# A decoder layer on one core: w1 and w3 of the second SwiGLU by Strassen's seven block products for features 4 to 21

## The chip, the cores and the metric

The kernel runs on one core of one Trainium2 chip. The metric is the device time of one execution in microseconds (us), as the median of several runs; lower is better.

## What is computed

One decoder layer on 512 tokens of 1024 features, float32 in and out. Two gated feed-forward blocks (SwiGLU) stand around a mixer of a diagonal state-space branch (S5) and a gated linear attention (GLA):

```python
def swiglu(x, w1, w3, w2):
    return (jax.nn.silu(x @ w1) * (x @ w3)) @ w2

h = h + 0.5 * swiglu(rms_norm(h, ffn1_norm[l]), ffn1_w1[l], ffn1_w3[l], ffn1_w2[l])
...
h = h + 0.5 * swiglu(rms_norm(h, ffn2_norm[l]), ffn2_w1[l], ffn2_w3[l], ffn2_w2[l])
out = rms_norm(h, final_norm)
```

w1 and w3 are 1024 x 2816, that is 22 tiles of 128 features; w2 is 2816 x 1024. In what follows a *feature* is one of these 22 tiles.

## The kernel before, in words

All activations lie feature-major: 128 features on the partitions, the 512 tokens along the row, so h is eight tiles of 128x512. Each float32 operand is split into two parts, `hi` (the value rounded to TensorE's format, written by ScalarE) and `lo` (the rest, subtracted by VectorE), and a product is three passes on TensorE: hi by hi, hi by lo and lo by hi (`mm3`, L208). `gemm` (L213) adds these over the tiles of the contraction into one PSUM bank.

The weights come as a stream of *units* (class `Unit`): one piece of 128x1024 or less, with its load on the SP queue, its split, its products (`mm`) and what follows on the other engines (`post`). The main loop (L1298) goes through the units in the order of the list and for each one issues the load of the unit five ahead, the products, the split of the unit three ahead, and the post. This loop is what sets the order on every engine: each engine works off its own queue in that order and waits by semaphores. There are five load buffers (`raw`), four `hi`, four `lo`, four PSUM banks `mm`, four `sp`, and 63 slots of 128x512 (`g`) for everything else.

`ffn` (L249) writes the units of a SwiGLU. For each feature there is a unit of w1 and one of w3, 24 products of 128x512 each (8 tiles by three passes); `g_post` (L253) makes the gate: two multiplications by the norm's factor out of PSUM, Silu on ScalarE, their product, its hi and lo. The second SwiGLU goes through the features in groups of 6, 6, 6 and 4 (`GROUPS2`). After each group come eight units of w2, one per tile of h, which add that group's share to h. The last group goes half of the tokens after half, with products of 128x256 (`tail_units`, L1166), since the final norm of the first half then runs beside the products of the second. Helpers record most operations, so VectorE's two-operand operations have L65, its scalar-tensor-tensor ones L77, ScalarE's L86, and TensorE's three passes L209 to L211.

Of the kernel before, what the change touches and what calls it, by code (L numbers as in the profile page):

```python
# [15 lines left out]
P = 128  # L16
# [4 lines left out]
GROUPS2 = [6, 6, 6, 4]  # L21
# [11 lines left out]
class Ring:  # L33
    def __init__(self, items):
        self.items = items
        self.n = 0

# [23 lines left out]
def _body(nc, a, sb, pp):  # L61
# [63 lines left out]
    def newton(y, v, t):  # L125
        """y = 1 / sqrt(v)."""
# [50 lines left out]
    def finish_h(m, g, norm):  # L177
        """hi and lo of h g for the next product, and the sum of squares; the DVE's share one tile later."""
# [40 lines left out]
    units = []  # L219

    def load(n):
# [3 lines left out]
        u.raw = raws.get()  # L225
        if u.load is not None:
            u.load(u)
        else:
            nc.sync.dma_start(out=u.raw[:, 0:u.width], in_=u.src)

    def split(n):
# [3 lines left out]
        if u.split is not None:  # L235
            u.split(u)
            return
# [3 lines left out]
        sub(u.lo[:, 0:w], u.raw[:, 0:w], u.hi[:, 0:w].bitcast(F32))  # L241

# [6 lines left out]
    def ffn(w1, w3, w2, groups, norm_key, lead, finish_tile, tail=False):  # L249
# [15 lines left out]
        for q, nk in enumerate(groups):  # L265
            last = q == len(groups) - 1
            for f in range(c0, c0 + nk):
# [17 lines left out]
                ua.early = ub.urgent and tail and last  # L285
                units.extend([ua, ub])
            if tail and last:
                tail_units(w2, c0, nk, gs)
                continue
            for m0 in range(0, KT, 2):  # L290
# [45 lines left out]
    for _ in range(WARM):  # the tensor engine's clock is at half until it has worked for a while  # L336
        PE.matmul(bank[:, 0:P], lhsT=idle, rhs=idle, start=True, stop=True)

    def lead1(ua, ub, pa, pb):
# [3 lines left out]
        ua.load = ub.load = no  # L343
# [3 lines left out]
        def mm():  # L347
            for u in (ua, ub):
                u.hi, u.lo = his.get(), los.get()
# [1025 lines left out]
```

## Time and profile before

| | |
|---|---|
| median of three runs | 1089.84 us (1089.45 to 1090.64) |
| span of the profiled execution, first to last instruction | 1085.4 us |
| the profiled execution's own time | not listed beside its span; the median is 4.4 us above the span |
| TensorE busy | 1070.3 us, 4968 products |
| VectorE busy | 626.8 us |
| ScalarE busy | 384.0 us |
| GpSimd busy | 68.8 us |
| mean granted TensorE clock | 0.994 of full speed |

How to read it: the span is what the profiler saw of one execution. Products are pipelined and their ends are modelled, so a single one is recorded longer (some 390 ns for 128x512) than the distance between two starts; what a product costs in a stream is the distance of the starts. The second SwiGLU takes about the last 375 us of the span.

### The profile page before, as it was taken

What the parts mean: (1) busy time and instruction counts of PE and PEld (TensorE: products, weight loads), DVE (VectorE), ACT (ScalarE), POOL (GpSimd) and SP (SyncE); (2) the same over time, 40 slices, a digit from 0 to 9 for tenths busy, and PEclk for the clock granted to TensorE, in tenths of its full rate; (3) what the DMA queues carried; (4) which work ended last, traced back from release to release, by engine and by line L of the source; (5) the groups of instructions that cost most, each with busy time, mean ns of one, the idle gap of its engine ahead of it and who ended that gap; (6) DMA issues with size and microseconds to landing.
All of it is one profiled execution on the core that took longest, in us unless ns stands there. A gap on an engine that the chain in (4) does not pass through costs nothing.

```text
span 1085.4 us, 12968 instructions
## 1 busy us (share of the span) xinstructions
PE 1070.3 (99%) x4968; PEld 892.2 (82%) x4968; DVE 626.8 (58%) x1164; ACT 384.0 (35%) x605; POOL 68.8 (6%) x121
## 2 busy tenths in 40 slices
PE   9999999999999999999999999999999999999996
PEld 7888888888888898888788888888888888888885
DVE  6688654896643637685585654655344444444446
ACT  6323254222222532654644333433222222322224
POOL 4003500100400000001000000000000000000001
PEclk9999999999999999999999999999999999999998
DMA  7323223421521332122131323323242233314112
GB/s 275 102 62 128 96 79 88 134 75 49 169 74 49 131 98 84 52 79 78 59 98 59 98 96 97 98 80 90 81 136 88 63 122 98 97 45 151 59 39 78
DMA packets 33228, 101.31 MB, mean 93 GB/s; under 512 B 3968, under 2 KB 5440, under 8 KB 33168
## 3 DMA queue, kind: packets, MB, share of 16 engines
q1 hardware_dynamic: 32256, 99.17, 28.9%
q0 software_dynamic: 480, 0.79, 0.3%
q8 instruction: 39, 0.64, 0.2%
q10 hardware_dynamic: 432, 0.54, 0.1%
q14 instruction: 21, 0.17, 0.1%
HBM read 98.19 MB, written 2.10 MB: 92 GB/s over the span
## 4 chain that ended last, share of the span: by engine, by line
PE 95%; ACT 2%; DVE 2%; DMA 1%; issue 0%; SPq 0%; DVEq 0%; ACTq 0%
PE mm L209 28%; PE mm L211 28%; PE mm L210 28%; ACT g L86 1%; DVE g L65 1%; PE sp L949 1%; PE sp L951 1%; PE sp L950 1%; PE mm L951 1%; PE mm L950 1%; PE mm L949 1%; PE sp L209 1%; PE sp L210 1%; PE sp L211 1%; ACT b L86 1%; DMA g<-x 1%
## 5 line engine op out<-in xcount | busy, mean ns | idle before, releaser
L209 PE MATMUL mm<-g,hi 128*128 128x512 f32 x1344 | 532.0, 396 | 0.0
L211 PE MATMUL mm<-g,lo 128*128 128x512 f32 x1344 | 526.3, 392 | 0.0
L210 PE MATMUL mm<-g,hi 128*128 128x512 f32 x1344 | 524.3, 390 | 0.0
L65 DVE TENSOR_TENSOR lo<-raw,hi 128x1024 fp32r<-128x1024 f32 (+3 forms) x200 | 221.5, 1112 | 167.2 <-ACT hi L86 166.1
L211 PEld LDWEIGHTS mm<-g,lo 128*128 128x128 f32 x1344 | 252.7, 188 | 58.4
L210 PEld LDWEIGHTS mm<-g,hi 128*128 128x128 f32 x1344 | 252.9, 188 | 53.9
L209 PEld LDWEIGHTS mm<-g,hi 128*128 128x128 f32 x1344 | 253.0, 188 | 51.9
L86 ACT ACTIVATE hi<-raw 128x1024 fp32r<-128x1024 f32 (+3 forms) x200 | 190.0, 959 | 207.2 <-PE mm L210 134.5
L86 ACT ACTIVATE g<-g 128x512 f32<-128x512 f32 (+3 forms) x184 | 112.4, 617 | 402.1 <-DVE g L65 401.9
L65 DVE TENSOR_TENSOR g<-g,g 128x512 f32<-128x512 f32 (+7 forms) x307 | 169.9, 571 | 50.6 <-ACT g L86 42.7
L65 DVE TENSOR_TENSOR g<-g,mm 128x512 f32<-128x512 f32 (+1 forms) x92 | 57.1, 637 | 54.8 <-PE mm L211 54.5
L77 DVE SCALAR_TENSOR_TENSOR g<-mm,g 128x512 f32<-128x512 f32 x45 | 30.9, 688 | 99.0 <-PE mm L211 99.0
L65 DVE TENSOR_TENSOR g<-mm,g 128x512 f32<-128x512 f32 x66 | 45.3, 686 | 26.5 <-PE mm L211 23.6
L86 ACT ACTIVATE g<-sp 128x128 f32<-128x128 f32 (+3 forms) x76 | 28.5, 405 | 40.0 <-PE sp L136 11.7
L1233 POOL TENSOR_TENSOR g<-g,g 128x512 f32<-128x512 f32 x4 | 5.4, 1380 | 538.4 <-ACT g L86 538.4
L558 POOL COPY g<-g 64x64 f32<-64x64 f32 x64 | 24.3, 380 | 57.6 <-DVE g L65 54.8
L65 DVE TENSOR_TENSOR g<-g 128x16 f32<-128x16 f32 (+1 forms) x132 | 24.1, 205 | 6.6 <-POOL g L558 3.8
L77 DVE SCALAR_TENSOR_TENSOR g<-g,vec,g 128x512 fp32r<-128x512 f32 (+1 forms) x28 | 21.0, 749 | 11.4 <-ACT g L86 11.2
L86 ACT ACTIVATE g<-g,vec 128x512 fp32r<-128x512 f32 (+1 forms) x40 | 23.7, 625 | 4.9 <-DMA g<-x 3.7
L86 ACT ACTIVATE b<-g 64x256 f32<-64x256 f32 x24 | 9.5, 413 | 19.3 <-DVE g L65 19.2
L65 DVE TENSOR_TENSOR g<-sp,g 128x512 f32<-128x512 f32 x21 | 13.4, 683 | 4.9 <-ACT g L86 3.2
L86 ACT ACT_TABLE_LOAD x10 | 12.8, 1283 | 1.4 <-PEq L1367 1.3
(151 smaller groups left out, 540.7 us busy)
## 6 DMA issues: line engine op xcount, KB each, us to landing
raw<-win SPq DMA_DIRECT2D x24, 512.0 KB, 3.4
raw<-w1b SPq DMA_DIRECT2D x22, 512.0 KB, 3.4
raw<-w3b SPq DMA_DIRECT2D x22, 512.0 KB, 3.4
raw<-w1a SPq DMA_DIRECT2D x21, 512.0 KB, 3.6
raw<-w3a SPq DMA_DIRECT2D x21, 512.0 KB, 3.5
raw<-w2b SPq DMA_DIRECT2D x24, 384.0 KB, 3.2
raw<-w2a SPq DMA_DIRECT2D x16, 384.0 KB, 3.1
raw<-w2a SPq DMA_DIRECT2D x16, 320.0 KB, 2.9
```

What stands on the lines that cost most here:

```text
L65: V.tensor_tensor(out=out, in0=x, in1=y, op=op)
L77: V.scalar_tensor_tensor(out=out, in0=x, scalar=s, in1=y, op0=op0, op1=op1)
L86: S.activation(out, x, f, **kw)
L209: PE.matmul(out, lhsT=wh, rhs=xh, start=start, stop=False)
L210: PE.matmul(out, lhsT=wh, rhs=xl, start=False, stop=False)
L211: PE.matmul(out, lhsT=wl, rhs=xh, start=False, stop=stop)
L558: G.tensor_copy(xv[half, :, gg, 3 - j, :], v3(src)[rows, 4 * b:4 * b + 4])
L949: PE.matmul(banks[i], lhsT=xh, rhs=wh, start=(k == 0), stop=False)
L950: PE.matmul(banks[i], lhsT=xh, rhs=wl, start=False, stop=False)
L951: PE.matmul(banks[i], lhsT=xl, rhs=wh, start=False, stop=(k == KT - 1))
L1233: (V if half else G).tensor_tensor(out=v3, in0=v3, in1=b3, op=ALU.mult)
```

## The change

Features 0 to 3 of the second SwiGLU stay as they were. For features 4 to 21, w1 and w3 of one feature together are taken as a 2x2 block matrix (w1 above w3; the first 512 input features beside the last 512), and the normalised x as a 2x2 block matrix too (first and last 512 input features; left and right 256 tokens). Instead of eight block products there are seven (in Winograd's form of Strassen's scheme), each of four tiles of the contraction by three passes, all 128x256: 84 products of 128x256 for 48 of 128x512. For that

- `seven_x` makes, during features 1 to 3 and the first pieces of w2, the normalised x and its seven combinations with hi and lo, on VectorE and ScalarE;
- `feature` makes four sums of the weights' blocks for each feature (`sums_a`, `sums_b`), splits those and the blocks themselves (`halve`: 3584 columns instead of 2048), and puts the products in the order 1, 2, 6, 5, 7, 4, 3. Products 1, 6, 7 and 4 add up in one PSUM bank, of which ScalarE copies the state after 1, 6 and 7 (`post_1`, `post_6`, `post_7`); products 5 and 3 add up in another. The outputs are combined on VectorE (`post_2`, `post_7`, `post_3`), go through Silu in halves and make the gate in halves;
- w2 no longer follows in blocks: its units are cut in two, and these half pieces (of the group before) stand between the products: in features 4 to 9 after products 7 and 4, in features 10 to 21 after 2, 5, 7 and 4. The groups become 4, 6, 4, 4 and 4. Half pieces use the `sp` banks, and the factor 0.5 moves to their addition to h;
- loads and splits of all this are entries of two lists with a due unit (`fetches`, `tasks`), worked off by `run_tasks` after the products of each unit and ahead of its post; the rings of buffers give out free ones (`take`, `drop`).

The diff, cut to its core:

```diff
--- before.py
+++ after.py
-GROUPS2 = [6, 6, 6, 4]
+GROUPS2 = [4, 6, 4, 4, 4]
...
     def split(n):
...
-        u.hi, u.lo = his.get(), los.get()
+        u.hi, u.lo = his.take(), los.take()
         w = u.width
         act(u.hi[:, 0:w], u.raw[:, 0:w], AF.Copy)
         sub(u.lo[:, 0:w], u.raw[:, 0:w], u.hi[:, 0:w].bitcast(F32))
+        raws.drop(u.raw)
+        u.raw = None
...
+    tasks, fetches = [], []
+
+    def run_tasks(n):
+
+        for queue in (fetches, tasks):
+            while queue and queue[0][0] <= n and all(r.room() for r in queue[0][1]):
+                queue.pop(0)[2]()
...
+    def step(mm, post=None):
+        u = Unit(None, 0, mm, post, split=nothing, load=nothing)
+        units.append(u)
+        return len(units) - 1
...
     def tail_rows(m, bank):
...
-            add(x[m % 4][:, HALVES[m // 4]], h[m][:, c], bank[:, c])
+            stt(x[m % 4][:, HALVES[m // 4]], bank[:, c], 0.5, h[m][:, c], ALU.mult, ALU.add)
...
+            i = step(lambda m=m: first(m), second if m == KT - 1 else post)
+            if m % 2 == 0:
+                fetches.append((i - 12, [raws], lambda m=m: fetch(m)))
+            tasks.append((i - 6, [], lambda m=m: hold(m)))
...
+    def seven_x(norm):
...
+        def made_of(p, k, src, sign):
+            xh, xl = X[p][0][k], X[p][1][k]
+            act(xh, src, AF.Copy, scale=sign)
+            stt(xl, src, sign, xh.bitcast(F32), ALU.mult, ALU.subtract)
...
+        for k in range(4):
+            for kk in (k, k + 4):
+                xn[kk] = get()
+                stt(xn[kk], h[kk], g2[:, kk:kk + 1], b, ALU.mult, ALU.mult)
+            made_of("1", k, xn[k][:, left], -1.0)
+            made_of("2", k, xn[k + 4][:, left], 1.0)
+            yield
...
+        for kp in range(2):
+            t1, t2[kp] = get(), get()
+            for i in range(2):
+                k = 2 * kp + i
+                sub(t1[:, HALVES[i]], xn[k][:, right], xn[k][:, left])
+                sub(t2[kp][:, HALVES[i]], xn[k + 4][:, right], t1[:, HALVES[i]])
+            for i in range(2):
+                made_of("6", 2 * kp + i, t2[kp][:, HALVES[i]], 1.0)
+            for i in range(2):
+                made_of("5", 2 * kp + i, t1[:, HALVES[i]], 1.0)
+            yield
...
+        for k in range(4):
+            made_of("3", k, xn[k + 4][:, right], -1.0)
+        yield
...
+        def parts(q):
...
+                    i = step(mm, post if z == 1 else None)
+                    if z == 0:
+                        fetches.append((i - 11, [raws], fetch))
+                        tasks.append((i - 4, [his, los], halve))
+                    yield
...
+            def product(p, bank, key, start):
+                wh, wl = w[key]
+                xh, xl = X[p]
+                for k in range(4):
+                    c = slice(k * P, (k + 1) * P)
+                    PE.matmul(bank, lhsT=wh[:, c], rhs=xh[k], start=start and k == 0, stop=False,
+                              skip_group_check=True)
+                    PE.matmul(bank, lhsT=wh[:, c], rhs=xl[k], start=False, stop=False, skip_group_check=True)
+                    PE.matmul(bank, lhsT=wl[:, c], rhs=xh[k], start=False, stop=k == 3, skip_group_check=True)
...
+            def sums_a():
+                v["s1"], v["s2"] = get(), get()
+                add(v["s1"], w["r3"][:, 0:T], w["r3"][:, T:2 * T])
+                add(v["s2"], v["s1"], w["r1"][:, 0:T])
+
+            def sums_b():
+                v["s4"] = get()
+                add(v["s4"], w["r1"][:, T:2 * T], v["s2"])
+                add(w["r3"][:, 0:T], w["r3"][:, 0:T], w["r1"][:, 0:T])
+                raws.drop(w["r1"])
+
+            def s_post():
...
+                mul(g[:, right], v["c22"], v["s"][:, right])
...
+                act(gh[:, c], g[:, c], AF.Copy)
+                late.append(lambda: sub(gl[:, c], g[:, c], gh[:, c].bitcast(F32)))
...
+            def post_1():
+                v["c1"] = get()
+                act(v["c1"][:, left], al, AF.Copy)
+                later()
...
+            def post_2():
+                v["x1"], v["s"] = get(), get()
+                sub(v["x1"][:, left], v["c1"][:, left], be)
+                act(v["s"][:, left], v["x1"][:, left], AF.Silu, scale=-1.0)
+                later()
...
+            def post_6():
+                v["u2"] = get()
+                act(v["u2"][:, left], al, AF.Copy)
...
+            def post_7():
+                v["u3"], v["c22"] = v["u2"], v["c1"]
+                act(v["u2"][:, right], al, AF.Copy)
+                v["c22"] = get()[:, left]
+                add(v["c22"], ga, v["u2"][:, right])
...
+                mul(v["g"][:, left], al, v["s"][:, left])
...
+            def post_3():
+                x = v["x1"]
+                add(x[:, right], ga, v["u2"][:, left])
+                act(v["s"][:, right], x[:, right], AF.Silu, scale=-1.0)
...
+            i = step(mm_1, post_1)
+            fetches.append((i - 9, [raws], lambda: fetch("r1", w1[f])))
+            fetches.append((i - 9, [raws], lambda: fetch("r3", w3[f])))
+            tasks.append((i - 4, [his, los], lambda: halve("a", ["a11", "a12"], [w["r1"]])))
+            step(mm_2, post_2)
+            take(0)
+            i = step(mm_6, post_6)
+            tasks.append((i - 5, [], sums_a))
+            tasks.append((i - 4, [his, los], lambda: halve("s12", ["s2", "s1"], [v["s2"], v["s1"]])))
+            tasks.append((i - 3, [], sums_b))
+            step(mm_5)
+            take(1)
+            i = step(mm_7, post_7)
+            tasks.append((i - 4, [his, los], lambda: (halve("s3a", ["s3", "a22"], [w["r3"]]), raws.drop(w["r3"]))))
+            take(2)
+            step(mm_4, post_4)
+            take(3)
+            i = step(mm_3, post_3)
+            tasks.append((i - 4, [], lambda: halve("s4_", ["s4"], [v["s4"]])))
...
+                places = {2, 3} if q == 1 else {0, 1, 2, 3}
+                feature(f, lambda i: next(fill) if i in places else None, f == NFF - 1)
...
-    f2 = ffn(a["w1b"], a["w3b"], a["w2b"], GROUPS2, "n2", lead2, None, tail=True)
+    f2 = ffn_seven(a["w1b"], a["w3b"], a["w2b"], GROUPS2, "n2", lead2)
...
+    for n, times in ((3, 2), (4, 2), (5, 1), (6, 1), (7, 1), (8, 1), (9, 2)):
+        side(f2 + n, *[xgen] * times)
...
         if n >= 1 and not u.urgent:
             split(n + 3)
+        run_tasks(n)
         if u.post is not None:
             u.post()
```

What this does to the order of the queues is shown at three places.

**VectorE, features 1 and 2.** Before, behind the gate of feature 1 (the multiplications out of `mm_91` and `mm_88`; `lo` is a split of weights):

```order
L65 TENSOR_TENSOR g_5289<-mm_91,g_5249 128x512
L77 SCALAR_TENSOR_TENSOR g_5291<-mm_88,g_5249 128x512
L65 TENSOR_TENSOR g_5289<-g_5291,g_5290 128x512
L65 TENSOR_TENSOR g_5297<-g_5289,g_5296 128x512
L65 TENSOR_TENSOR lo_73<-raw_67,hi_69 128x1024
L65 TENSOR_TENSOR lo_74<-raw_63,hi_70 128x1024
L65 TENSOR_TENSOR g_5354<-mm_89,g_5249 128x512
```

And of the change, at the same place:

```order
L83 TENSOR_TENSOR g_5292<-mm_91,g_5251 128x512
L83 TENSOR_TENSOR g_5294<-mm_88,g_5251 128x512
L83 TENSOR_TENSOR g_5292<-g_5294,g_5293 128x512
L83 TENSOR_TENSOR g_5300<-g_5292,g_5299 128x512
L95 SCALAR_TENSOR_TENSOR g_5305<-g_96,vec,g_5251 128x512
L95 SCALAR_TENSOR_TENSOR g_5307<-g_100,vec,g_5251 128x512
L95 SCALAR_TENSOR_TENSOR b_5303<-g_5305,b_5303 128x256
L95 SCALAR_TENSOR_TENSOR b_5304<-g_5307,b_5304 128x256
L95 SCALAR_TENSOR_TENSOR g_5313<-g_97,vec,g_5251 128x512
L95 SCALAR_TENSOR_TENSOR g_5315<-g_101,vec,g_5251 128x512
L95 SCALAR_TENSOR_TENSOR b_5303<-g_5313,b_5303 128x256
L95 SCALAR_TENSOR_TENSOR b_5304<-g_5315,b_5304 128x256
```

The combinations of x (`g_96` to `g_103` are h) now stand between one gate and the next split of weights; this goes on in the same way up to the first half pieces of w2.

**VectorE, feature 5 to feature 6.** Before, a feature in this queue is two splits and a gate, as in the first block above. Of the change, from what follows product 7 (`mm_91` holds products 5 and 3) to the split for the next feature's product 7 (`raw_65` and `raw_66` are the next feature's w1 and w3, `sp_92` a piece of w2):

```order
L83 TENSOR_TENSOR g_5803<-mm_91,g_5771 128x256
L83 TENSOR_TENSOR lo_72<-raw_65,hi_68 128x1024
L83 TENSOR_TENSOR g_5825<-raw_66 128x512
L83 TENSOR_TENSOR g_5826<-g_5825,raw_65 128x512
L83 TENSOR_TENSOR g_5829<-mm_89,g_5756 128x256
L83 TENSOR_TENSOR lo_73<-g_5826,hi_69 128x512
L83 TENSOR_TENSOR lo_73<-g_5825,hi_69 128x512
L95 SCALAR_TENSOR_TENSOR g_99<-sp_92,g_99 128x512
L83 TENSOR_TENSOR g_5856<-raw_65,g_5826 128x512
L83 TENSOR_TENSOR raw_66<-raw_66,raw_65 128x512
L83 TENSOR_TENSOR g_5755<-mm_91,g_5771 128x256
L83 TENSOR_TENSOR lo_74<-raw_66,hi_70 128x1024
```

Work on this feature's products (out of `mm_91`, `mm_89`) and on the next one's weights alternate in one queue.

**ScalarE at the same place.** Before, for a feature: Silu, hi of the gate, two splits.

```order
L86 ACTIVATE g_5290<-g_5289 128x512
L86 ACTIVATE g_5296<-g_5289 128x512
L86 ACTIVATE hi_69<-raw_67 128x1024
L86 ACTIVATE hi_70<-raw_63 128x1024
L86 ACTIVATE g_5355<-g_5354 128x512
```

Of the change, from the split of the two sums for products 6 and 5 (`hi_69`) to the copy after product 7 of feature 6, whose bank is `mm_88`:

```order
L104 ACTIVATE hi_69<-g_5826 128x512
L104 ACTIVATE hi_69<-g_5825 128x512
L104 ACTIVATE g_5756<-g_5755 128x256
L104 ACTIVATE hi_70<-raw_66 128x1024
L104 ACTIVATE g_5877<-mm_88 128x256
L104 ACTIVATE g_5830<-g_5829 128x512
L104 ACTIVATE hi_71<-raw_67 128x512
L104 ACTIVATE g_5897<-g_5896 128x256
L104 ACTIVATE g_5912<-mm_88 128x256
L104 ACTIVATE g_5939<-g_5856 128x512
L104 ACTIVATE g_5912<-mm_88 128x256
```

The three copies out of `mm_88`, for which TensorE's next product into that bank waits, stand behind a Silu of the feature before (`g_5756`), a split that needs VectorE's last sum (`hi_70`), the hi of the gate (`g_5830`) and a Silu of this feature (`g_5897`).

## Rows read from the trace of the kernel before

**Rows 1.** The head of the page: span, and busy time of the engines.
```profile
span 1085.4 us, 12968 instructions
PE 1070.3 (99%) x4968; PEld 892.2 (82%) x4968; DVE 626.8 (58%) x1164; ACT 384.0 (35%) x605; POOL 68.8 (6%) x121
```
**Rows 2.** Busy times by stretch: one feature of the second SwiGLU.
```profile
751.00:762.00 11.00, 11.00 (x50) 9.03 (x49) 4.86 (x6) 3.06 (x4) 0.00 (x0) 1.00 0.35 102
```
**Rows 3.** Timeline of TensorE at the end of the second SwiGLU: start, length.
```profile
1034.71 0.39 PE L209 MATMUL mm<-g,hi 128*128 128x512 f32 x1
...
1048.90 0.40 PE L211 MATMUL mm<-g,lo 128*128 128x512 f32 x1
...
1052.00 0.28 PE L209 MATMUL mm<-g,g 128*128 128x256 f32 x1
...
1060.64 0.28 PE L209 MATMUL sp<-g,g 128*128 128x256 f32 x1
```
**Rows 4.** Groups by form, weight loads: count, busy us, mean ns, idle.
```profile
L209 PEld LDWEIGHTS mm<-g,g 128*128 128x128 f32 x32 | 6.1, 192 | 0.0
```
**Rows 5.** Groups by form, VectorE, from 700 us on.
```profile
L65 DVE TENSOR_TENSOR lo<-raw,hi 128x1024 fp32r<-128x1024 f32 x43 | 52.7, 1225 | 43.8 <-ACT hi L86 43.4
L65 DVE TENSOR_TENSOR g<-g,g 128x512 f32<-128x512 f32 x28 | 19.4, 692 | 3.3 <-ACT g L86 0.8 <-DVE g L77 0.5
L65 DVE TENSOR_TENSOR g<-g,mm 128x256 f32<-128x256 f32 x16 | 5.9, 417 | 12.0 <-PE mm L211 12.0
```
**Rows 6.** Groups by form, ScalarE, from 700 us on.
```profile
L86 ACT ACTIVATE hi<-raw 128x1024 fp32r<-128x1024 f32 x42 | 44.2, 1054 | 76.2 <-PE mm L210 50.6 <-issue 25.6
L86 ACT ACTIVATE g<-g 128x512 f32<-128x512 f32 x28 | 17.7, 632 | 57.3 <-DVE g L65 57.3
L86 ACT ACTIVATE g<-g 128x256 f32<-128x256 f32 x8 | 3.2, 415 | 5.0 <-DVE g L65 5.0
```
**Rows 7.** Timeline of VectorE: five operations on end, and two.
```profile
1052.13 3.09 DVE L65 TENSOR_TENSOR g<-raw,g 128x512 fp32r<-128x512 f32 x5
...
1066.18 0.75 DVE L65 TENSOR_TENSOR g<-g,sp 128x256 f32<-128x256 f32 x2
```
**Rows 8.** Timeline of ScalarE: five on end; two starts of 256 columns.
```profile
1051.40 2.70 ACT L86 ACTIVATE g<-raw 128x512 fp32r<-128x512 f32 x5
...
1068.77 0.39 ACT L86 ACTIVATE g<-mm 128x256 f32<-128x256 f32 x1 [0.43 <-PE mm L136]
1069.05 0.41 ACT L86 ACTIVATE g<-g 128x256 f32<-128x256 f32 x1
```
**Rows 9.** Timeline of all engines: the gate of one feature.
```profile
741.71 0.69 DVE L77 SCALAR_TENSOR_TENSOR g<-mm,g 128x512 f32<-128x512 f32 x1 [2.75 <-PE mm L211]
...
742.50 0.69 DVE L65 TENSOR_TENSOR g<-g,g 128x512 f32<-128x512 f32 x1
...
743.23 0.63 ACT L86 ACTIVATE g<-g 128x512 fp32r<-128x512 f32 x1 [3.61 <-DVE g L65]
...
743.89 0.69 DVE L65 TENSOR_TENSOR g<-g,g 128x512 fp32r<-128x512 f32 x1 [0.70 <-ACT g L86]
```
**Rows 10.** Timeline of TensorE: at the start, and around its longest wait.
```profile
8.40 0.50 PE L209 MATMUL sp<-g,hi 128*128 128x512 f32 x1 [0.75 <-ACT hi L86]
...
538.02 1.16 PE L854 MATMUL sp<-g,g 64*128 64x128 f32 x8 [2.45 <-ACT g L86]
...
539.68 0.55 PE L211 MATMUL mm<-g,lo 128*128 128x512 f32 x1
540.03 0.63 PE L209 MATMUL mm<-g,hi 128*128 128x512 f32 x1
...
543.32 0.39 PE L211 MATMUL mm<-g,lo 128*128 128x512 f32 x1
```
**Rows 11.** Busy times by stretch there; the granted clock is third from the end.
```profile
540.00:542.00 2.00, 2.00 (x6) 1.58 (x5) 1.62 (x3) 1.43 (x2) 0.00 (x0) 0.50 0.00 0
```
**Rows 12.** The page's DMA issues: KB each, us to landing.
```profile
raw<-w1b SPq DMA_DIRECT2D x22, 512.0 KB, 3.4
```

More of the change, by code (lines that the diff above doesn't have):

```diff
@@ L41, in get, with room, take, drop @@
         return t
+    def room(self):
+        return len(self.held) < len(self.items)
+    def take(self):
+        while self.n % len(self.items) in self.held:
+            self.n += 1
+        i = self.n % len(self.items)
+        self.held.add(i)
+        self.n += 1
+        return self.items[i]
+    def drop(self, t):
+        for i, x in enumerate(self.items):
+            if x is t:
+                self.held.discard(i)
 class Unit:
@@ L228, in load @@
         else:
+            u.raw = raws.take()
             nc.sync.dma_start(out=u.raw[:, 0:u.width], in_=u.src)
@@ L241, in split, with release, nothing @@
         sub(u.lo[:, 0:w], u.raw[:, 0:w], u.hi[:, 0:w].bitcast(F32))
+        raws.drop(u.raw)
+        u.raw = None
+    def release(u):
+        for ring, t in ((raws, u.raw), (his, u.hi), (los, u.lo)):
+            if t is not None:
+                ring.drop(t)
+        u.raw = u.hi = u.lo = None
+    tasks, fetches = [], []
[3 more added lines that the diff above has]
+                queue.pop(0)[2]()
+    def nothing(u=None):
+        return None
+    def step(mm, post=None):
+        u = Unit(None, 0, mm, post, split=nothing, load=nothing)
+        units.append(u)
+        return len(units) - 1
     h = [get() for _ in range(KT)]
@@ L341, in no, with only_room @@
             return None
-        ua.load = ub.load = no
+        def only_room(u):
+            u.raw = raws.take()
+        ua.load = ub.load = only_room
         ua.split = ub.split = no
@@ L348, in mm @@
             for u in (ua, ub):
-                u.hi, u.lo = his.get(), los.get()
+                u.hi, u.lo = his.take(), los.take()
             pa[0], pb[0] = spps.get(), spps.get()
@@ L1169, in tail_units, with fetch, hold @@
         banks, sqs, out = [], [[], []], [[], []]
-        def hold(u):
+        def fetch(m):
+            u, v = us[m], us[m + 1]
+            u.raw = raws.take()
             w = u.width
+            for i, x in enumerate((u, v)):
+                nc.sync.dma_start(out=u.raw[:, i * w:(i + 1) * w], in_=x.src)
+        def hold(m):
+            u, r = us[m], us[m // 2 * 2].raw
+            w = u.width
+            x = r[:, m % 2 * w:(m % 2 + 1) * w]
             u.hi, u.lo = pair()
-            act(u.hi[:, 0:w], u.raw[:, 0:w], AF.Copy)
-            sub(u.lo[:, 0:w], u.raw[:, 0:w], u.hi[:, 0:w].bitcast(F32))
+            act(u.hi[:, 0:w], x, AF.Copy)
+            sub(u.lo[:, 0:w], x, u.hi[:, 0:w].bitcast(F32))
+            if m % 2:
+                raws.drop(r)
         def product(half, m, ks):
@@ L1264, in second @@
             result(1, mmps.get())
-        for m, u in enumerate(us):
-            u.split = hold
-            u.mm = lambda m=m: first(m)
+        for m in range(KT):
+            post = None
             if 4 <= m < KT - 1:
-                u.post = lambda m=m: (rows(0, m - 4), gather(m - 5) if m > 5 else None)
-        us[-1].post = second
-        units.extend(us)
-    f2 = ffn(a["w1b"], a["w3b"], a["w2b"], GROUPS2, "n2", lead2, None, tail=True)
-    at_lead(f2, "n2", 1)
+                post = lambda m=m: (rows(0, m - 4), gather(m - 5) if m > 5 else None)
+            i = step(lambda m=m: first(m), second if m == KT - 1 else post)
+            if m % 2 == 0:
+                fetches.append((i - 12, [raws], lambda m=m: fetch(m)))
+            tasks.append((i - 6, [], lambda m=m: hold(m)))
@@ L1301, in _body @@
         u.mm()
+        if n >= 1:
+            release(units[n - 1])
         if n == 1:
@@ L1314, in _body @@
             next(gen, done)
-    for gen in (prep, s5, gl):
+    for gen in (prep, s5, gl, xgen):
         assert next(gen, done) is done
```

183 lines of the change are left out of this document (172 added, 11 removed).

## The prediction

> **What bounds the kernel now.** The head of the page first: TensorE is busy 1070.3 us of a span of 1085.4, VectorE 626.8 [rows 1]. A busy TensorE need not be at its peak, so next the busy times of one stretch of the second SwiGLU: in 11 us TensorE shows no gap, while VectorE works 4.86 us and ScalarE 3.06 [rows 2]. The timeline of TensorE tells the price of a product: 62 steps from 1034.71 to 1048.90 make 228.9 ns for each 128x512, 72 steps from 1052.00 to 1060.64 make 120.0 ns for each 128x256 [rows 3]. A 128x256 so costs 52.4% of a 128x512. The weight load is recorded with 192 ns beside those 120 ns steps [rows 4], so loads overlap, and a load for half as many columns doesn't bind. The stage is bound by the count of its products.
>
> **The change part by part.** The order of the changed kernel has 1512 products of 128x256 (18 features, 84 each) for 864 of 128x512; that it does what it says is therefore not in doubt. *Products:* 864 x 0.2289 = 197.8 us go, 1512 x 0.1200 = 181.4 us come: **-16.3 us** if nothing else is late. The products of w2 are the same in number and width; only their place moves. By the Trainium skill ("TensorE: Matmul & The Clock Gate", Back-to-back issue gap) an isolated product takes N/2.4 + 2.5 ns, 215.8 and 109.2 ns; the trace shows some 11 to 13 ns more in both, and by the page the saving would be 21.4 us. The sum goes by the rows.
>
> *VectorE and ScalarE* get the price. For each of the 18 features the weights' sums (four adds of 512 columns), high and low parts of 3584 columns for 2048, and five operations of 256 columns on the partial sums. Durations, as recorded: VectorE 1.225 us for 1024 columns, 0.69 for 512, 0.42 for 256 [rows 5]; ScalarE 1.054, 0.632 and 0.39 to 0.415 [rows 6]. Where the next one doesn't need the result of the one before, it starts sooner: five low parts took 3.09 us, so 0.60 each (2.40 between starts and 0.69 for the last), two operations of 256 columns 0.75, so 0.34, and 1024 columns, by the same 0.09 less, 1.14 [rows 7]; on ScalarE 0.52 for 512 columns and 0.28 for 256 [rows 8]. A hand-over between the two engines takes the whole duration and 0.03 us; on one engine a dependent operation starts 0.10 after the end [rows 9]. VectorE's own work in one feature: 2 x 1.14, 8 x 0.60, 5 x 0.34, and one piece of w2 (0.60 split, 0.60 evacuation): 10.0 us. In features 4 to 9 (two half pieces of w2 each) TensorE needs 84 x 0.120 + 12 x 0.2289 = 12.8 us, so the work would fit. **What doesn't fit is the order.** Both queues run in order and hand work to each other, and one feature's chain of hand-overs has to be through before the next one's.
>
> I walk it from the end of the third block product in place (7) to the same in the next feature, with these durations. ScalarE's copy of the bank starts at 0; its high part of the next feature's first weights 0.28 to 1.33, VectorE's low part from 1.36; the first sum at 2.50, the second, which needs it, 3.29 to 3.98; ScalarE's high part of it to 4.64; the two low parts from 4.67 and 5.27; the evacuation of w2 at 5.87; two more sums from 6.47 and 7.07; the addition on the last product 7.67 to 8.09; ScalarE's Silu at 8.12 and, behind it, the high part of the sums for product 7, 8.40 to 9.45; its low part on VectorE from 9.48; the multiplication 10.62 to 11.04; ScalarE's high part of g to 11.70; the low part of g from 11.73, w2's from 12.33, the subtraction for Silu 12.93 to 13.35; ScalarE's Silu at 13.38, and only then its copy of the bank after product 6, 13.66 to 14.06. Product 7 adds to that bank, so it waits for this copy; it takes 1.44 and its end is seen 0.16 later. **One turn takes 15.7 us, TensorE's own work 12.8: 2.9 us lost per feature**, half in front of product 6 (ScalarE's copy of product 1 stands behind the high part that ends at 9.45), half in front of product 7. For features 5 to 9 that is 5 x 2.9 = **+14.6 us**. From feature 10 on two whole pieces of w2 lie in each feature: TensorE needs 18.3 us (10 to 13) and 15.6 us (14 to 21), while the same walk gives some 14.3 to 14.9, so nothing is lost there, the margin at 15.6 being under 1 us.
>
> *Before feature 4* VectorE also has to make seven combinations of x. From the end of feature 1's last product its queue holds: three gates of features 1 to 3, at 3.4 each with their waits for ScalarE (2.87 from 741.71 to the end of the last operation, and 0.60 for the multiplication ahead [rows 9]); the combinations, 4 x 2.1 + 4 x 2.8 + 1.4 = 21.0 (in each of the first four steps two 512 products 0.60 apart, then two differences that wait for ScalarE's copies); four splits of weights, each behind ScalarE's copy, 5.4; sums and halves of feature 4 3.7; two evacuations 1.2; the rest, up to ScalarE's copy of product 1, 0.9: 42.4 us. TensorE reaches product 6 of feature 4 after 4 x 5.49 + 4 x 1.37 + 2 x 1.44 = 30.3 us. **+12.1 us**, about 5 of it in front of the second half piece of w2 (which needs feature 3's gate) and 7 in front of product 6.
>
> *The clock.* In the mixer TensorE stood still for 2.45 us; soon after, products were 0.63 us long for 0.39 and the granted clock was 0.50, its lower level of 1.2 GHz; nine products from 539.68 to 543.32 took 3.64 us where nine steps of 0.229 make 2.06 [rows 10, 11]: 1.6 us lost. The two long waits will do the same; after the first the loss lies inside the second wait, after the second it counts: **+1.6 us**. Whether the waits of 1.5 us do it no row shows. The nearest are 0.75 us, behind which products took 0.50 and none 0.63, and 2.45 [rows 10]: between nothing and 1.44 us for each turn, product 7 at half the clock. I take nothing, since 1.5 is nearer to 0.75 than to 2.45.
>
> *The rest.* The loads by SP move as many bytes in smaller pieces and are issued eight or nine units ahead; they land 3.4 us after issue [rows 12]. The buffer that waits longest, the next w3, is free when the two later sums are through and is read some 10 us later: nothing. The end of the kernel keeps its steps; the eight splits of the last pieces (0.60 each on VectorE) fall into features with a margin, and the last gate is now made for one half of the tokens first: nothing, at worst 2 us.
>
> Sum: -16.3 + 14.6 + 12.1 + 1.6 = +12.0, span 1097.4. The profile gives only the span; 4.4 us lie between it and the median of 1089.84, and I keep them: **1102 us**.
>
> **Rivals.**
> 1. *The two engines keep up* (the other sign). For it: 10.0 us of VectorE's work for 12.8 of TensorE's, and splits that the code issues four units ahead of their product. If the turn stays under 12.8 us and the combinations of x are through in time, only the products count: 1073.5. It decides at the length of the turn. Against it: the turn has a row's duration in each of its steps, and every step needs the one before, by data or by its place in a queue.
> 2. *The turn is shorter by a tenth,* because recorded ends lie later than what the next engine waits for: 14.2 us, and 38 for 42.4: +6.9 and +7.8, about 1090 with the clock as it is. No row speaks for it; 0.03 us between end and start speaks against.
> 3. *The turn binds in features 14 to 21 too,* because it is a tenth longer (waits for buffers or semaphores that no row shows): 16.2 for 15.6 there, 17.3 for 12.8 before, about 42 us of waits: 1116.
> 4. *The clock falls after every wait of 1.5 us:* ten of them, product 7 slow in each of five turns, 5 x 1.44 = 7.2: 1109. For it the Trainium skill ("TensorE: Matmul & The Clock Gate", A second HAM failure mode: psum-queue depth-cycling): short idle times between groups of products can let the clock fall and rise again and cost throughput. The rows agree only for a longer wait.
>
> **Numbers.** The forecast 0.55, rival 1 0.13, rival 2 0.09, rival 3 0.10, rival 4 0.13. The range 1088 to 1113 leaves out rivals 1 and the worse part of 3; its lower end is rival 2 with the clock untouched, its upper end rival 4 with steps 5% longer. A measurement of this kernel can tell about 0.2% from no change, 2.2 us: faster is under 1087.7 (rival 1 and a little of 2), 0.15; the same 0.07; slower 0.78.
>
> **What would show it.** Right: VectorE nearly without a free moment from feature 1's end to feature 4; a wait of TensorE of about 5 us in the second piece of w2 and of 7 in front of product 6 of feature 4, both for ScalarE or VectorE; then starts of product 1 in steps of 15.7 us in features 4 to 9, with two waits near 1.5 us in each, in steps of 18.3 in 10 to 13 and 15.6 after; a granted clock of 0.5 behind the long wait. Products of 128x256 in steps of 0.120 between the waits. Wrong: steps of 12.8 us in features 5 to 9 (then the walk is wrong, rival 1), or steps above 15.6 in the last eight (rival 3).

## The result, and the profile after

The changed kernel takes **1098.07 us** (median of four runs, 1096.97 to 1098.85), the kernel before, beside it, 1089.64 (1088.61 to 1090.64): ratio 1.0084, 95% interval 1.0069 to 1.0100. It is slower, as forecast, by 8.4 us where some 12 were expected.

The head of the page of the changed kernel, which answers to [rows 1]:

```profile
span 1095.3 us, 14607 instructions
...
PE 1055.0 (96%) x5616; PEld 908.6 (83%) x5616; DVE 726.6 (66%) x1395; ACT 441.9 (40%) x768; POOL 68.9 (6%) x121
```

TensorE is busy 15.3 us less than in [rows 1], and the span is 9.9 longer: 25.2 us of waits have come in. The list of TensorE's waits says for whom. The columns are: waiting engine, tile and line, the engine and line waited for, us in total, times, longest.

```profile
PE mm L1487 <- ACT g L104: 19.4, 11, 5.4
PE sp L227 <- ACT g L104: 4.7, 1, 4.7
PE sp L895 <- ACT g L104: 2.5, 1, 2.5
PE mm L1268 <- DVE g L83: 2.4, 1, 2.4
PE mm L154 <- DVE stat L95: 2.2, 1, 2.2
PE sp L227 <- ACT hi L104: 1.8, 3, 1.1
PE sp L375 <- DVE idle L372: 1.2, 1, 1.2
```

The 2.5, 2.4, 2.2 and 1.2 stand in the kernel before as well. The first, second and sixth line are new but for 0.7 us: 19.4 + 4.7 + 1.8 - 0.7 = 25.2. The sixth line's three waits lie in the first 11 us of the kernel, far ahead of the change, and cost nothing in the end: the wait in the mixer ends at 538.08 us here and at 538.02 in [rows 10]. So 24.1 us of waits belong to the change, all of them for ScalarE (which waits for VectorE in its turn, as rows below show). L1487 is the first of the three passes of a block product, and it waits for the bank.

Where they are, in the timeline of TensorE (start, length; in brackets the idle time ahead and its releaser). L227 is a half piece of w2; of the rows with a wait, `mm<-b,hi` is product 6 and `mm<-g,hi` product 7.

```profile
759.46 0.80 PE L227 MATMUL sp<-g,hi 128*128 128x512 f32 x1 [4.66 <-ACT g L104]
...
774.23 0.58 PE L1487 MATMUL mm<-b,hi 128*128 128x256 f32 x1 [5.37 <-ACT g L104]
...
790.70 0.38 PE L1487 MATMUL mm<-b,hi 128*128 128x256 f32 x1 [1.53 <-ACT g L104]
...
795.06 0.39 PE L1487 MATMUL mm<-g,hi 128*128 128x256 f32 x1 [1.27 <-ACT g L104]
...
806.60 0.38 PE L1487 MATMUL mm<-b,hi 128*128 128x256 f32 x1 [1.47 <-ACT g L104]
...
810.97 0.38 PE L1487 MATMUL mm<-g,hi 128*128 128x256 f32 x1 [1.28 <-ACT g L104]
...
822.51 0.38 PE L1487 MATMUL mm<-b,hi 128*128 128x256 f32 x1 [1.53 <-ACT g L104]
...
882.29 0.28 PE L1487 MATMUL mm<-g,g 128*128 128x256 f32 x1
...
900.25 0.28 PE L1487 MATMUL mm<-g,g 128*128 128x256 f32 x1
```

Two long waits, one in the half pieces of w2 ahead of feature 4 and one in front of its product 6; then two short ones per feature, and a turn of 15.91 us (790.70 to 806.60 to 822.51). The last two lines are product 3 of two neighbouring features of the group 10 to 13: 17.96 us apart, and nothing waits.

Busy times by stretch (length; PE, PEld, DVE, ACT, POOL with their counts; then granted clock, DMA share, GB/s). The stretches are: features 2 and 3 (first two lines), up to feature 4, then features 5 to 9, 10 to 13, 14 to 21. Two short stretches follow, around the end of the first wait and behind the second.

```profile
731.00:742.00 11.00, 11.00 (x49) 9.03 (x49) 9.37 (x16) 4.15 (x8) 0.00 (x0) 1.00 0.14 48
742.00:753.00 11.00, 11.00 (x49) 9.03 (x49) 9.55 (x21) 5.16 (x12) 0.00 (x0) 1.00 0.09 24
753.00:765.00 12.00, 7.34 (x20) 5.26 (x19) 10.62 (x25) 5.27 (x12) 0.00 (x0) 0.73 0.13 44
...
780.00:870.00 90.00, 75.99 (x555) 70.64 (x554) 60.93 (x98) 36.56 (x68) 0.00 (x0) 1.00 0.22 74
870.00:945.00 75.00, 75.00 (x507) 68.96 (x506) 51.62 (x80) 32.54 (x58) 0.00 (x0) 1.00 0.31 106
945.00:1060.00 115.00, 115.00 (x815) 107.35 (x814) 90.12 (x154) 53.00 (x100) 0.00 (x0) 1.00 0.31 104
...
759.00:761.00 2.00, 1.54 (x3) 1.01 (x4) 1.56 (x4) 0.82 (x2) 0.00 (x0) 0.50 0.00 0
...
775.00:777.00 2.00, 2.00 (x12) 2.00 (x11) 1.09 (x3) 0.42 (x1) 0.00 (x0) 0.50 0.85 326
```

Beside features 2 and 3 VectorE works 9.4 of 11 us where it worked 4.86 [rows 2]. From 780 to 870 TensorE stands still for 14 us, and no engine is full: VectorE is busy 68%, ScalarE 41%. From 870 to 1060 TensorE has no gap.

The hand-over itself, in the timeline of all engines, from the Silu of feature 4 to the two products of feature 5 that wait:

```profile
789.01 0.42 ACT L104 ACTIVATE g<-g 128x256 f32<-128x256 f32 x1 [2.97 <-DVE g L83]
789.34 1.04 ACT L104 ACTIVATE hi<-raw 128x1024 fp32r<-128x1024 f32 x1
790.28 0.36 ACT L104 ACTIVATE g<-mm 128x256 f32<-128x256 f32 x1
790.41 1.23 DVE L83 TENSOR_TENSOR lo<-raw,hi 128x1024 fp32r<-128x1024 f32 x1 [1.43 <-ACT hi L104]
...
791.55 0.42 DVE L83 TENSOR_TENSOR g<-g,g 128x256 f32<-128x256 f32 x1
...
792.00 0.63 ACT L104 ACTIVATE g<-g 128x512 fp32r<-128x512 f32 x1 [1.36 <-DVE g L83]
...
792.66 0.69 DVE L83 TENSOR_TENSOR g<-g,g 128x512 fp32r<-128x512 f32 x1 [0.70 <-ACT g L104]
...
793.27 0.69 DVE L83 TENSOR_TENSOR lo<-raw,hi 128x512 fp32r<-128x512 f32 x1
...
793.87 0.41 DVE L83 TENSOR_TENSOR g<-g,mm 128x256 f32<-128x256 f32 x1
...
794.32 0.42 ACT L104 ACTIVATE g<-g 128x256 f32<-128x256 f32 x1 [1.17 <-DVE g L83]
794.64 0.36 ACT L104 ACTIVATE g<-mm 128x256 f32<-128x256 f32 x1
```

The two `g<-mm` on ScalarE are its copies after product 1 and after product 6; TensorE starts product 6 at 790.70 and product 7 at 795.06, 0.06 us behind their ends. Ahead of the second copy the engines take turns: VectorE waits 1.43 and 0.70 us for ScalarE, ScalarE 1.36 and 1.17 for VectorE. Each is idle while the other works, and the copy that TensorE waits for stands at the end of the row.

### The profile page after: what moved, and what is told of

Its sections match the earlier page's. It is cut to its first block, busy times and chain, and to the rows that moved or that the text cites. A ratio compares the mean times of both kernels' runs of the same rounds, so it can differ in the third digit from the quotient of the medians.

```text
span 1095.3 us, 14607 instructions
## 1 busy us (share of the span) xinstructions
PE 1055.0 (96%) x5616; PEld 908.6 (83%) x5616; DVE 726.6 (66%) x1395; ACT 441.9 (40%) x768; POOL 68.9 (6%) x121
## 4 chain that ended last, share of the span: by engine, by line
PE 84%; DVE 8%; ACT 5%; issue 1%; DMA 1%; SPq 0%; DVEq 0%; ACTq 0%
PE mm L227 18%; PE mm L228 18%; PE mm L229 18%; PE mm L1487 4%; PE mm L1490 4%; PE mm L1489 4%; DVE g L83 4%; PE sp L228 3%; PE sp L229 3%; PE sp L227 3%; DVE lo L83 3%; ACT g L104 2%; ACT hi L104 2%; DVE g L95 1%; PE sp L990 1%
## 5 line engine op out<-in xcount | busy, mean ns | idle before, releaser
L227 PE MATMUL mm<-g,hi 128*128 128x512 f32 x912 | 361.5, 396 | 0.0
L228 PE MATMUL mm<-g,hi 128*128 128x512 f32 x912 | 357.1, 392 | 0.0
L229 PE MATMUL mm<-g,lo 128*128 128x512 f32 x912 | 356.9, 391 | 0.0
L83 DVE TENSOR_TENSOR lo<-raw,hi 128x1024 fp32r<-128x1024 f32 (+4 forms) x208 | 221.6, 1074 | 155.4 <-ACT hi L104 154.8
L104 ACT ACTIVATE g<-g 128x512 f32<-128x512 f32 (+4 forms) x237 | 132.9, 569 | 349.2 <-DVE g L83 336.9
L104 ACT ACTIVATE hi<-raw 128x1024 fp32r<-128x1024 f32 (+4 forms) x208 | 189.3, 928 | 108.8 <-PE mm L228 64.5
L83 DVE TENSOR_TENSOR g<-g,g 128x512 fp32r<-128x512 f32 (+7 forms) x338 | 181.7, 555 | 57.6 <-ACT g L104 51.7
L227 PEld LDWEIGHTS mm<-g,hi 128*128 128x128 f32 x912 | 171.7, 188 | 36.1
L228 PEld LDWEIGHTS mm<-g,hi 128*128 128x128 f32 x912 | 171.8, 188 | 35.8
L83 DVE TENSOR_TENSOR g<-mm,g 128x256 f32<-128x256 f32 (+1 forms) x106 | 58.0, 550 | 36.4 <-PE mm L229 16.9
L1487 PE MATMUL mm<-b,hi 128*128 128x256 f32 x216 | 61.4, 284 | 12.9 <-ACT g L104 12.9
L227 PE MATMUL sp<-g,hi 128*128 128x512 f32 x160 | 64.0, 400 | 6.5 <-ACT g L104 4.7
L1487 PE MATMUL mm<-g,hi 128*128 128x256 f32 x216 | 60.8, 281 | 6.5 <-ACT g L104 6.5
L228 PE MATMUL sp<-g,hi 128*128 128x512 f32 x160 | 64.2, 401 | 0.0
L1489 PE MATMUL mm<-b,hi 128*128 128x256 f32 x216 | 60.6, 281 | 0.0
L1489 PE MATMUL mm<-g,hi 128*128 128x256 f32 x216 | 60.2, 279 | 0.0
L83 DVE TENSOR_TENSOR g<-g,mm 128x512 f32<-128x512 f32 (+1 forms) x74 | 45.0, 616 | 15.4 <-PE mm L229 15.3
L1487 PEld LDWEIGHTS mm<-b,hi 128*128 128x128 f32 x216 | 41.1, 190 | 14.6 <-ACT g L104 14.1
```

Source lines behind the costliest of these rows:

```text
L83: V.tensor_tensor(out=out, in0=x, in1=y, op=op)
L104: S.activation(out, x, f, **kw)
L227: PE.matmul(out, lhsT=wh, rhs=xh, start=start, stop=False)
L228: PE.matmul(out, lhsT=wh, rhs=xl, start=False, stop=False)
L229: PE.matmul(out, lhsT=wl, rhs=xh, start=False, stop=stop)
L1487: PE.matmul(bank, lhsT=wh[:, c], rhs=xh[k], start=start and k == 0, stop=False, skip_group_check=True)
```

## The experiments

The theory is that of the prediction: TensorE waits for the *order* of the hand-overs (a turn of 15.7 us where TensorE has 12.8 of work) and, once, for the combinations of x. Its rival is the *amount*: VectorE and ScalarE have too much to do.

**e1: the same work, w2's half pieces two products earlier.** In features 4 to 9 they stand after products 2 and 5 instead of 7 and 4.

```diff
-                places = {2, 3} if q == 1 else {0, 1, 2, 3}
+                places = {0, 1} if q == 1 else {0, 1, 2, 3}
```

> One word of the order: in features 4 to 9 the two half pieces of w2 stand after products 2 and 5 instead of 7 and 4; work, splits and loads are the same. The order theory (a turn of hand-overs between ScalarE and VectorE that TensorE waits for in front of products 6 and 7): the piece after 2 covers ScalarE's copy of product 1, the piece after 5 its copy of product 6; the walk with the durations of before gives a turn of 13.4 us instead of 15.7 (12.8 would be TensorE's own), so some 13 us less, about 1085, and waits in front of 6 and 7 of under 0.2 us in features 5 to 9. The amount theory (VectorE has too much to do in features 4 to 9, wherever TensorE waits): the waits move to other products, time within 2 us of 1098.

Measured: 1080.67 us (1080.62 to 1080.97), ratio 0.9939 (0.9924 to 0.9954). Not one operation less, and now 0.6% *faster* than before, by 4 us more than the order theory said. In features 5 to 9 products 6 and 7 no longer wait. What is left is one wait of 0.47 us in front of product 4, which the expectation did not have; it comes every 13.1 us:

```profile
793.83 0.38 PE L1487 MATMUL mm<-g,hi 128*128 128x256 f32 x1 [0.47 <-ACT g L104]
...
806.95 0.38 PE L1487 MATMUL mm<-g,hi 128*128 128x256 f32 x1 [0.47 <-ACT g L104]
```

VectorE, in the 90 us from 780, is busier than in the change, since it gets further:

```profile
780.00:870.00 90.00, 87.16 (x651) 82.03 (x651) 71.26 (x117) 42.83 (x79) 0.00 (x0) 1.00 0.30 94
```

So the engines can do this work in TensorE's time; it was the order. A half piece between products 2 and 6 covers the copy for which product 6 waits, one between 5 and 7 the copy for product 7. Product 4 now follows product 7 directly and waits for the copy in between. The gain is not in the turns alone: five of them, 2.78 us shorter each, make 13.9 us, and the wait in front of product 6 of feature 4 fell from 5.37 to 1.65 us.

**e2: without the normalised x and its combinations.** `seven_x` takes existing tiles instead; the making of the normalised x and of its seven combinations is left out of the computation.

```diff
     def seven_x(norm):
...
-        b = norm.b
-
-        def made_of(p, k, src, sign):
...
+        for p, c in zip("1265743", (left, right) * 4):
+            X[p] = [xs[k][0][:, c] for k in range(4)], [xs[k][1][:, c] for k in range(4)]
+        yield
```

> Left out: the normalised x and its seven combinations; the products read parts of the eight tiles that ordinary features use. Everything else is as in the changed kernel. If VectorE's queue ahead of feature 4 is what costs, the waits of 4.7 and 5.4 us there shrink to about 2.3 and 0.4 and the slow clock behind them goes: 9.4 us by the walk and 1.6 for the clock, about 1087. If these waits have another cause (a late load, the norm), it stays within 3 us of 1098. Features 5 to 9 keep their steps of 15.7 to 15.9 us in both cases.

Measured: 1085.49 us (1084.16 to 1086.43), ratio 0.9978 (0.9969 to 0.9988); span 1082.5, 12.8 under the change. Of the two long waits 0.4 us are left where 2.7 were expected; the turns stay at 15.9 us (starts of product 6 at 777.80, 793.71 and 809.62). So the combinations of x cause the long waits and not the turns.

**e5: both at once.** e1's and e2's edits together; the same part is left out as in e2.

> Both cuts together: half pieces of w2 after products 2 and 5 in features 4 to 9, and the normalised x and its seven combinations left out (the products read parts of the ordinary tiles). If the two costs are what eats the saving, they add up: 16 us (measured alone) and 11 us less than the changed kernel, so 1070 to 1073, which is the saving of the products, 16.3 us under the kernel before, less some 0.5 us of waits per feature in 5 to 9. If one hides the other, it stays at 1078 to 1081.

Measured: 1069.89 us (1069.02 to 1072.31), ratio 0.9845 (0.9825 to 0.9864). Against the span of the change e1 gives 16.3 us, e2 12.8 and both 28.0 (1095.3 to 1067.3): they nearly add up, to 29.1. They overlap at the second long wait, of which e1 takes 3.7 us as well. The result is 16.9 us under the kernel before, beside it (1086.79). That is not yet the bare saving of the products: the six features 4 to 9 still have a wait of 0.47 us each in front of product 4, and the two waits ahead of feature 4 make 0.4 (the bare saving is worked out below).

**e3: less amount on VectorE.** The four sums of the weights' blocks of each feature go to GpSimd.

```diff
+    def gadd(out, x, y):
+        G.tensor_tensor(out=out, in0=x, in1=y, op=ALU.add)
...
-                add(v["s1"], w["r3"][:, 0:T], w["r3"][:, T:2 * T])
-                add(v["s2"], v["s1"], w["r1"][:, 0:T])
+                gadd(v["s1"], w["r3"][:, 0:T], w["r3"][:, T:2 * T])
+                gadd(v["s2"], v["s1"], w["r1"][:, 0:T])
...
-                add(v["s4"], w["r1"][:, T:2 * T], v["s2"])
-                add(w["r3"][:, 0:T], w["r3"][:, 0:T], w["r1"][:, 0:T])
+                gadd(v["s4"], w["r1"][:, T:2 * T], v["s2"])
+                gadd(w["r3"][:, 0:T], w["r3"][:, 0:T], w["r1"][:, 0:T])
```

> The four sums of weights of each Strassen feature (512 columns each) are made by GpSimd instead of VectorE; VectorE has 2.4 us less to do per feature, 24% of its work in features 4 to 9. GpSimd took 1.38 us for such a multiplication of 512 columns before, against 0.69. The order theory: the sums stay links of the turn, and slower ones; turn about 16.0 for 15.7, time 1097 to 1100. The amount theory: 2.4 us less in each of features 5 to 9 and less of a queue before 4, so 10 to 14 us less, 1084 to 1088.

Measured: 1094.31 us, ratio 1.0062 (1.0047 to 1.0077): in neither range, between the two, nearer to that of the order theory. The turn became 15.2 to 15.7 us where the walk said 16.0, so here the walk missed: by it the slower sums lengthen the turn, and it became shorter. Groups by form from 780 to 870 us (count, then busy us and mean ns, then idle time ahead), VectorE and GpSimd of e3:

```profile
L83 DVE TENSOR_TENSOR lo<-raw,hi 128x1024 fp32r<-128x1024 f32 x12 | 18.0, 1499 | 11.7 <-ACT hi L107 11.7
L83 DVE TENSOR_TENSOR lo<-g,hi 128x512 fp32r<-128x512 f32 x12 | 16.8, 1434 | 0.0
...
L83 DVE TENSOR_TENSOR g<-mm,g 128x256 f32<-128x256 f32 x18 | 7.5, 417 | 5.3 <-ACT g L107 4.9 <-PE mm L1493 0.2
...
L92 POOL TENSOR_TENSOR g<-g,raw 128x512 f32<-128x512 f32 x6 | 11.6, 1930 | 0.5
```

The sums (the POOL row is one of the four) take 1.4 to 1.9 us there for 0.69 on VectorE, and VectorE's low parts beside them take 1434 ns where the change shows 689. So e3 does not take the amount away cleanly: part of what left VectorE came back as longer operations. It is weak evidence by itself. By the Trainium skill ("SBUF — State Buffer", SBUF: two separate sides) VectorE operations with two SBUF inputs and GpSimd operations that read SBUF exclude each other for the whole instruction; the rows agree, the low parts (two inputs from SBUF) are the ones that grew, while those that read one operand from a bank kept their 0.42 us (7.5 us for 18).

**e6: one hand-over out of the turn.** The split of the next feature's first weights (for products 1 and 2) is issued one unit earlier.

```diff
-            tasks.append((i - 4, [his, los], lambda: halve("a", ["a11", "a12"], [w["r1"]])))
+            tasks.append((i - 5, [his, los], lambda: halve("a", ["a11", "a12"], [w["r1"]])))
```

> One number: the split of w1's two blocks for the next feature's products 1 and 2 falls due one unit earlier, so that in both queues it stands ahead of the copy and the addition after product 7 instead of behind them. The same work. The order theory: the split no longer lies in the turn after product 7 but beside the wait for it; the walk gives 14.4 us for 15.7, about 6 us less, 1092. The amount theory: no difference, 1098 within 2 us.

Measured: 1091.52 us (1089.97 to 1092.68), ratio 1.0038 (1.0023 to 1.0052). The turn is 14.61 us (starts of product 7 at 795.64, 810.25 and 824.86) for a walked 14.4, with a wait of 1.28 in front of product 7 and one of some 0.2 in front of product 6. One entry of the order, with the same operations, is worth 1.3 us a turn.

**e8: the cover of features 10 to 21 taken away.** There the four half pieces of w2 stand together behind product 3.

```diff
             i = step(mm_3, post_3)
             tasks.append((i - 4, [], lambda: halve("s4_", ["s4"], [v["s4"]])))
+            if f >= sum(GROUPS2[:2]):
+                for k in range(4):
+                    place(k)
```

(`take`, between the products, does nothing in these features.)

> The changed kernel, but in features 10 to 21 the four half pieces of w2 stand together behind product 3 of the feature instead of after products 2, 5, 7 and 4; features 4 to 9 are untouched and nothing is left out. Order theory: in the change these features lose nothing because the pieces between the products give ScalarE and VectorE time for the copies and splits that the next product needs; together, they cover the way from product 3 to the next product 1 alone, and the seven products meet the hand-overs uncovered. By the walk with the durations of the kernel before, a turn of features 10 to 13 takes some 19.0 us for the 18.0 measured, of features 15 to 21 some 18.4 for 15.2: with TensorE's own work as it is, about 26 us more, 1124 us (range 1108 to 1132), with waits of TensorE for ScalarE in each of features 10 to 21 in front of products 6 and 7. Amount theory (with all the work of a feature inside TensorE's time, the place of the pieces is free): turns of 18.0 and 15.2 as they are, 1098 us.

Measured: 1130.55 us (1128.88 to 1131.23), ratio 1.0388 (1.0371 to 1.0406): 6.5 us more than expected, inside the range given. The timeline of its TensorE in one of the features 15 to 21:

```profile
965.51 0.38 PE L1489 MATMUL mm<-b,hi 128*128 128x256 f32 x1 [1.05 <-ACT g L104]
...
969.79 0.39 PE L1489 MATMUL mm<-g,hi 128*128 128x256 f32 x1 [1.19 <-ACT g L104]
...
971.94 0.39 PE L1489 MATMUL mm<-g,hi 128*128 128x256 f32 x1 [0.47 <-ACT g L104]
```

Products 6, 7 and now 4 wait, in a turn of 18.77 us (15.21 in the change; 18.4 walked). In features 11 to 14 product 4 alone waits, 0.47 us, and the turn is 18.83 (walked 19.0). So these features lose nothing in the change because the pieces stand *between* the products.

**e4: both causes out of the way, nothing left out.** Six features stay as they were, four groups of four follow, and every feature with block products has four half pieces between them; the combinations of x spread over features 2 to 5 and the first two block products, and no half piece stands ahead of the first block product.

```diff
-GROUPS2 = [4, 6, 4, 4, 4]
+GROUPS2 = [6, 4, 4, 4, 4]
...
-            fetches.append((i - 9, [raws], lambda: fetch("r1", w1[f])))
-            fetches.append((i - 9, [raws], lambda: fetch("r3", w3[f])))
+            due = max(i - 9, first + 2 * groups[0] - 5)
+            fetches.append((due, [raws], lambda: fetch("r1", w1[f])))
+            fetches.append((due, [raws], lambda: fetch("r3", w3[f])))
...
-            if q == 1:
-                for _ in range(4):
-                    next(fill)
-            left_, n = (12, 6) if q == 1 else (16, 4)
-            assert groups[q] == n
+            n = groups[q]
...
-                places = {2, 3} if q == 1 else {0, 1, 2, 3}
+                places = {0, 1, 2, 3}
...
-    for n, times in ((3, 2), (4, 2), (5, 1), (6, 1), (7, 1), (8, 1), (9, 2)):
+    for n, times in ((4, 1), (5, 1), (6, 1), (7, 1), (8, 1), (9, 1), (11, 1), (12, 1), (13, 2)):
```

> Groups of 6, 4, 4, 4, 4: features 4 and 5 stay with ordinary products, the combinations of x are spread over the time up to feature 6, one step after each unit, and every Strassen feature has four half pieces of w2 between its products. Nothing is left out. The order theory: the combinations find VectorE half idle (some 21 us of work in 55 us), and no feature with two pieces is left, so hardly any wait of TensorE remains; 16 features save 48 x 0.2289 - 84 x 0.1200 = 0.91 us each, 14.5 us, so 14 us under the kernel before: about 1074 to 1076. The amount theory (VectorE's work in Strassen features costs what it saves): within 3 us of the kernel before.

Measured: **1072.57 us** (1072.14 to 1073.89), ratio 0.9868 (0.9850 to 0.9885), faster than both kernels: 14.2 us under the kernel before, beside it (1086.79), for a saving of 16 features. Two waits are left of all those in features with block products, one in front of product 1 and one in front of product 7 of feature 6:

```profile
777.57 0.36 PE L1487 MATMUL mm<-b,hi 128*128 128x256 f32 x1 [2.68 <-ACT g L104]
790.19 0.39 PE L1487 MATMUL mm<-g,hi 128*128 128x256 f32 x1 [1.04 <-ACT g L104]
```

Feature 6 loses some 6 us by them: the first wait, and 21.13 us from its product 1 to that of feature 7, which takes 17.84; behind the 2.68 us the granted clock was 0.50 (779 to 781 us). VectorE makes combinations of x there, but no run tells whether they are the cause. By the steps measured below a feature saves 48 x 0.2289 - 84 x 0.1160 = 1.24 us where 0.91 was counted, 19.9 us for 16 features; less these 6 that is the 14.2, near the 14.5 expected by two errors that cancel.

**e0: the changed kernel once more,** beside e4 and e5, as their yardstick.

> The changed kernel once more, beside the others of this call, as their reference: 1096 to 1099, steps of 15.9 us from feature to feature in 5 to 9.

Measured: 1097.97 us, ratio 1.0097 (1.0076 to 1.0118).

## Why the prediction was right, step by step

Forecast 1102 us, measured 1098.07; the profiled span was forecast at 1097.4 and is 1095.3. The order of the queues was the reason, and it was foreseen as such: both long waits, the two short ones in every turn, and the stretch without a loss behind them. That the number came so near is in part luck, since two errors in it have opposite signs. The terms came out so:

- *Products, -16.3.* This is the mis-sized term: -22.4. The prediction took 0.120 us for each 128x256 product, from the end of the kernel [rows 3]. In the timeline of TensorE the steps of the 1469 block products that stand neither beside a wait nor in the slow clock average 0.1160, which makes 175.3 us for the 181.4 counted. (In features 10 to 21 alone it is 0.1157: 17.96 us less 36 products of 512 at 0.2289 leaves 9.72 for 84.) TensorE's busy time fell by only 15.3, because it holds losses as well: 5.2 us by products at a granted clock of 0.50 (the 15 of 512 columns from 759.46 to 765.87 took 6.40 us for 3.43, the 22 of 256 from 774.23 to 779.03 took 4.80 for 2.55), and 0.27 at each wait, since the last product ahead of it is recorded 0.16 longer than its step and the first behind it takes 0.11 more. The Trainium skill ("TensorE: Matmul & The Clock Gate", Back-to-back issue gap) has 109.2 ns for an isolated product; the measured step lies between that and [rows 3]. The estimate of the saving by the Trainium skill's figures, 21.4 us, is nearer to 22.4 than the prediction's sum, as both of its prices lie 6% under the measured steps.
- *The turn, +14.6* (5 x 2.9 is 14.5). 15.91 us for the walked 15.7, with two waits near the 1.5 foreseen; the ten waits of features 5 to 9 make 19.4 - 5.4 = 14.0. With the cheaper products TensorE's own work in a turn is 12.5 us for 12.8, so 3.4 are lost in each. The walk held where the hand-overs bind in other orders, too: 14.6 for 14.4 (e6), 18.8 for 18.4 (e8, features 15 to 21). In e3 it missed, 15.2 to 15.7 for 16.0. The 13.1 of e1 (for 13.4) and the 18.8 of e8's features 11 to 14 (for 19.0) do not test it: there the turn is TensorE's own work and one wait for a copy that starts as product 7 ends.
- *Before feature 4, +12.1.* Product 6 of feature 4 starts 21.65 us behind the start of the first piece of w2 (752.58 to 774.23), 13.3 more than TensorE's own work of 8.3; e2, without the combinations, is 12.8 shorter. The first wait is 4.66 for about 5, the second 5.37 for 7, since the slow products behind the first use up some of it.
- *The clock, +1.6.* About 0.6: from product 6 of feature 4 to that of feature 5, behind the second wait, it is 16.47 us (774.23 to 790.70), in the other turns 15.91. The step "after the second it counts" failed: product 7 of feature 4 would have waited some 1.3 us anyway (1.29 in e2), and most of the slow products' 2.2 us ran in that time.
- *Features 10 to 21, nothing.* Right, for the reason given (e8). 17.96 and 15.21 us stand for 18.3 and 15.6, by the shorter products.
- *What lies outside the span:* 2.8 us at this median for the 4.4 kept. A time is some 1.7 us above its own span (1096.97 and 1095.3); the rest is how far the profiled execution lay under the median.

From the first piece of w2 on, the change takes 10.1 us more than the kernel before: -22.4 by the products, +13.3 up to product 6 of feature 4, and +19.2 behind it, where turns and clock were forecast at 16.2. So the products were 6.1 us better than forecast and the waits 4.2 us worse. These errors cancel to 1.9 of the 3.9 us between forecast and result, and most of the rest lies outside the span. They are not independent: a cheaper product leaves TensorE more to wait in the same turn.

The rivals. *The engines keep up* fell with the turn of 15.91; e1 shows that moving the half pieces alone brings most of it about, so the rival was right about the amount of work. *A turn shorter by a tenth* fell with the same 15.91, *the turn binds in 14 to 21 too* with the 115 us without a gap. *The clock falls after every wait of 1.5 us* fell with the row from 780 to 870: ten waits of 1.27 to 1.53 us, and a granted clock of 1.00. Behind the waits of 4.66 and 5.37 us it was 0.50, and in e4 behind one of 2.68. The Trainium skill ("TensorE: Matmul & The Clock Gate", A second HAM failure mode) describes a clock that falls and rises with short idle times between groups of products; no run here shows it for waits of 1.5 us.

## What to carry to other kernels

Where two engines that each work off a queue in order hand work to each other, cost the turn of the hand-overs by walking both queues with recorded durations and compare it with the third engine's work in that turn; the sums of busy time (10.0 us for 12.8 here, 68% busy while TensorE waits) say nothing about it. Independent work of the waiting engine belongs directly in front of the instruction that waits: moving two half pieces of w2 by two products was worth 16 us on the span, and it turned a loss into a gain. Preparation that is done once still needs a stretch that hides it: the combinations of x cost 13 us because they met the first use too soon. When the first use came two features later (e4), some 6 us were still lost at that place, from whatever cause.

## What was not expected of the hardware

- *Products of 128x256 have no single price.* Timeline of TensorE of the change, from the start of product 6 to the end of product 5 (24 products), and of product 3 (12) and the beginning of product 1 behind it:

```profile
888.63 0.28 PE L1487 MATMUL mm<-b,hi 128*128 128x256 f32 x1
...
891.36 0.39 PE L227 MATMUL sp<-g,hi 128*128 128x512 f32 x1
...
900.25 0.28 PE L1487 MATMUL mm<-g,g 128*128 128x256 f32 x1
...
901.70 0.28 PE L1487 MATMUL mm<-b,hi 128*128 128x256 f32 x1
```

  24 in 2.73 us are 0.1137 each; the 12 of product 3 in 1.45 are 0.121. Products 1 and 2 behind product 3 take 0.1175. In e8, where no piece stands between, product 5 takes 0.1175, which had 0.1133 in the change. What sets it no run tells; this stays open.
- *GpSimd's help is dear.* In e3 VectorE's low parts of 128x512 took 1434 ns beside GpSimd's sums, 689 without, those of 128x1024 1499 for 1225; the expectation had not counted this.
